# Finishing the first expert's down products before the second expert's rows are transposed

## The chip, the cores and the metric

The kernel runs on one core of a Trainium2 chip. The metric is the device time of one execution in microseconds; three executions of the kernel before gave a median of 880.13 us, from 878.72 to 883.2. The trace was taken in another, profiled execution of the same program.

The core has five engines that the text names as the profile does: PE (TensorE, matrix products and transposes; PEld are its weight loads), DVE (VectorE), ACT (ScalarE), POOL (GpSimd) and SP (SyncE, which here only issues transfers). Each engine works through its own list of instructions in order, and an instruction whose inputs are not there holds up everything behind it on that engine.

## The reference

The model is one layer over 512 tokens of width 1024: a mixer (three linear-attention branches), a layer norm, then a mixture of experts and a last layer norm. The change touches the mixture alone. A router takes two of 16 experts for each token (both from one of four groups of experts), and the sum of the two experts' outputs, each weighted, goes on:

```python
h = jax.nn.silu(jnp.einsum('td,edf->tef', t, w_gate)) * jnp.einsum('td,edf->tef', t, w_up)
y = jnp.einsum('tef,efd->td', h * combine[..., None].astype(h.dtype), w_down)
```

An expert has two matrices of 1024 x 256 (gate, up) and one of 256 x 1024 (down), in float32: 3 MB per expert.

## The kernel before

Everything is float32. A product of full precision is made from three products of split operands: each matrix is split into a high part (a rounding copy by ACT, `L321`) and a low part (the rest, a subtraction by DVE, `L322`), and `mm3` (`L337` to `L339`) multiplies high x high, high x low and low x high into the same PSUM bank. The third product is the only one that reads the low part of the left operand.

The expert loop begins at `L1639`. For each expert `e` there are 128 slots, each a token that chose it. Four things happen, in four functions:

- `slots_of` (`L1591`, by way of `slots`, `L1487`) finds which token sits in which slot: DVE makes one-hot matrices (`L1496`), PE multiplies them with a small table (`L1498`), and DVE makes the indices for reading and writing rows, `gidx` and `sidx` (`L1502` to `L1504`). What it returns, `rest`, makes the weights of the slots, `wsl`, from the same one-hots: four small products per expert (`L1510`) and one reduction (`L1511`).
- `gather` (`L1525`) reads the tokens' rows from the DRAM copy `h1d` into SBUF by an indirect transfer that POOL issues; `ex_in` (`L1536`) transposes them on PE (eight transposes, `L1541`), and `parts` splits each half into high (ACT, `L1533`) and low (DVE, `L1534`).
- `ex_up` (`L1545`) multiplies the rows with the gate and up matrices: four steps `u` of six products of 512 columns. After step `u` it calls `hook[u]`, if there is one.
- `ex_down` (`L1573`) takes the up products through `ex_hidden` (`L1560`: Silu on ACT, times the slot's weight on DVE, two transposes on PE, a split), multiplies with the down matrix (two splits, twelve products), copies the outcome to SBUF (ACT, `L1582`) and writes the rows to `y2d` by an indirect transfer (`L1583`).

The first expert's rows are not gathered: they are picked out of the norm's output by one-hot products (`rows0`). The second expert is the first one whose rows come through `h1d`, and its gather can't begin until the last block of `h1d` is written.

The loop runs one expert behind with the down products. In the turn of `e` it issues up(`e`), then the fetch of `e + 1` (the gather of the rows of `e + 2` and the transposes of the rows of `e + 1`), and then down(`e - 1`). In the first turn there is no down; down(0) comes in the second turn, after up(1) and the transposes of the third expert's rows.

The order on each engine is made by a planner: it takes the instructions in the order of the program, and where one is not ready by its own reckoning it may take a later one that is. Two things bind it. An instruction of a `Pinned` engine (`W` for DVE, `TP` for PE; all of them have the line `L149` in the profile) stays behind the instruction traced before it on that engine. What stands in `tc.issue_after(i)` stays behind `i`. In the first turn `TE` is `TP`, so all of PE's work of that turn is in the order of the program. The splits of the second expert's gate and up matrices stand behind `lows`, the last split of the first expert's rows (`L1551`). The splits of the first expert's down matrix have no such tie.

The split matrices go through rings of five buffers (`whs`, `wls`). A split has to wait until the products that read the buffer's former content are done. The first expert's third and fourth up matrices use the first two buffers; before the change the next four splits are the second expert's.

The hooks of the first three turns put the making of slots into the up products: `slots23` (slots of the third and fourth expert, and `weighs`, small DVE work on the router's weights) after step 2 of the first, `weights03` (slots of the first expert, which it needs for its down products alone, and all weights `wsl`) after step 1 of the second.

Of the kernel before, what the change touches and what calls it, by code (L numbers as in the profile page):

```python
# [38 lines left out]
def kernel(  # L39
# [6 lines left out]
    V, S, G, TE = nc.vector, nc.scalar, nc.gpsimd, nc.tensor  # L46
# [89 lines left out]
    def flat(a):  # L136
        return a.rearrange("p a b -> p (a b)")
# [13 lines left out]
    def pst(pool, shape=(P, T)):  # L151
        return pool.tile(list(shape), F32, name="ps")
# [4 lines left out]
    if True:  # L157
# [44 lines left out]
        W, X, TP, GP, Y = (Pinned(e) for e in (V, S, TE, G, nc.sync))  # L202
# [208 lines left out]
    def after(f):  # L411

        if act[0] is None:
            i = f()
        else:
            with tc.issue_after(act[0].ins):
                i = f()
        act[0] = i
        return i
# [550 lines left out]
    def weave(a, b=None, lead=0, more=0):  # L970


        res, live, i = [None, None], [a, b] if b else [a], 0
        while live:
            for g in list(live):
                if g is a or i >= lead or a not in live:
                    try:
                        res[g is b] = next(g)
                        if g is (b or a):
                            fill(more, 8)  # L980
                    except StopIteration:
                        live.remove(g)
            i += 1
        return res
# [112 lines left out]
    oA0, _ = weave(m0, more=2)  # L1097
# [19 lines left out]
    oC1, _ = weave(diag("C1", *q1[1], *f1[1], [vC1], False), more=4)  # L1117
# [4 lines left out]
    oB, _ = weave(diag("B", *fB[1], vB, True), more=4)  # L1122
# [19 lines left out]
    E = 16  # L1142
# [56 lines left out]
    def wo_unit(ch, u, *hl):  # L1199
        raw = raws((P, 2, T))  # L1200
        nc.sync.dma_start(raw, dram(w_out, D * 256 * u + 512 * ch, [[D, P], [D * P, 2], [1, 512]]))
        return split(raw, *hl)
# [184 lines left out]
    def rows0(q, n0, n1):  # L1387

        for n in range(n0, n1):
            for c in range(4):  # L1390
                TE.matmul(xps[q][:, c * P:(c + 1) * P], ah[n][:, (4 * q + c) * P:(4 * q + c + 1) * P], oh0[:, n],
                          start=n == 0 and c == 0, stop=n == NT - 1 and c == 3)
# [24 lines left out]
    late = [wo_unit(1, 2, *x4[:2]), wo_unit(1, 3, *x4[2:])]  # L1417
# [33 lines left out]
    half, logits, scores, rows, _ = lns[3]  # L1451
    xps += [pst(pp) for _ in range(2)]
    made = act[0]
    W, TP = Pinned(V), TE
# [61 lines left out]
    xgs = []  # L1516
# [14 lines left out]
    def parts(xT, q, ps, V=V):  # L1531
        qs = slice(4 * q, 4 * q + 4)
        S.copy(flat(xT[0][:, qs]), ps)  # L1533
        return V.tensor_sub(flat(xT[1][:, qs]), ps, flat(xT[0][:, qs]).bitcast(F32))  # L1534

    def ex_in(xg):  # L1536
        xT = [xTs((P, KD, P), F32R), xTs((P, KD, P), F32R)]
        for q in range(2):
            ps = pst(pm)
            for c in range(4):  # L1540
                TE.transpose(ps[:, c * P:(c + 1) * P], xg[:, (4 * q + c) * P:(4 * q + c + 1) * P], ident)  # L1541
            parts(xT, q, ps)
        return xT
# [16 lines left out]
    def ex_hidden(ps, wcol):  # L1560
        sg = scr()
        S.activation(sg[:, 0:256], ps[:, 0:256], AF.Silu)
        V.scalar_tensor_tensor(sg[:, 256:], ps[:, 256:], wcol, sg[:, 0:256], op0=ALU.mult, op1=ALU.mult)
        ps = pst(pm)
        for c in range(2):
            TE.transpose(ps[:, c * P:(c + 1) * P], sg[:, 256 + c * P:256 + (c + 1) * P], ident)
        mh = scrp.tile([P, 2, 2, P], F32R, name="mh", tag="scr", bufs=4)
        hT_ = [mh[:, 0], mh[:, 1]]
        S.copy(flat(hT_[0]), ps[:, :256])
        sub = V.tensor_sub(flat(hT_[1]), ps[:, :256], flat(hT_[0]).bitcast(F32))  # L1570
        return hT_, sub

    def ex_down(ps, raw, wcol, sidx_col, m=2 * T, e=0, hidden=None):  # L1573
        hT_, sub = hidden or ex_hidden(ps, wcol)
        yo = yos((P, D))
        ps = [pst(pp), pst(pp)]
        for k in range(2):
            w = split(raw[4 + k], V=G if e == E - 1 and k == 1 else V)
            for c in range(2):
                mm3(ps[c], lambda b, k: hT_[b][:, k], lambda b, k: w[b][:, c], k, k + 1, k == 0, k == 1)  # L1580
        for c in range(2):
            S.copy(yo[:, c * T:(c + 1) * T], ps[c])  # L1582
        s = nc.gpsimd.indirect_dma_start(  # L1583
            out=y2d[:m], out_offset=bass.IndirectOffsetOnAxis(ap=sidx_col, axis=0), in_=yo, in_offset=None,
            bounds_check=m - 1, oob_is_err=False)
        for o in scats:
            tc.declare_no_dep(s.ins, o.ins, reason="rows of other slots")
        scats.append(s)
        return sub

    def slots_of(e0, e1, V=V, mid=None):  # L1591
        es = slice(e0, e1)
        return slots(range(e0, e1), lambda e: pos[:, :, e:e + 1], lambda n, e: rc[:, n, e], gidx[:, es], sidx[:, es], wsl[:, es], V, mid)
# [3 lines left out]
    def fetch(e):  # L1597
        wts = weights(e) if e > 1 else first[e]
        if e % 4 == 1 and 1 < e < E - 4:
            slots_of(e + 3, e + 7)()  # L1600
        if e < E - 1:
            gather(xgs[(e + 1) % 3], gidx[:, e + 1:e + 2])
        return wts, ex_in(xgs[e % 3])


    first.append(weights(1))
    xT = [xTs((P, KD, P), F32R), xTs((P, KD, P), F32R)]
# [6 lines left out]
    def low(u):  # L1614
        W.tensor_sub(ready[u][1], first[0][u], ready[u][0].bitcast(F32))

    rows0(0, 2, 4)
    rest = [slots_of(1, 2, W, lambda: low(2))]
    rows0(1, 2, 4)
    parts(xT, 0, xps[0], W)  # L1620
    gather(xgs[1], gidx[:, 1:2])
    low(3)
    lows = parts(xT, 1, xps[1], W)
    wts = first[0]

    def slots23():
        rest.append(slots_of(2, 4, W))
        for f in weighs:
            f()

    def weights03():
        with tc.issue_after(lows.ins):
            rest.append(slots_of(0, 1))
        for f in rest:
            f()

    hooks = [{2: slots23}, {1: weights03}, {1: lambda: slots_of(4, 8)()}] + [{} for _ in range(E - 3)]
    late = None
    for e in range(E):  # L1639
        if e == E - 1:  # L1640
            ex_down(*late, e=e - 1)
        TE = TP if e == 0 else nc.tensor
        hid = []
        if 1 < e < E - 1:
            hooks[e][2] = lambda: hid.append(ex_hidden(late[0], late[2]))
        ps = ex_up(xT, wts, ready if e == 0 else (), e, hooks[e])
        done = late
        late = ps, wts, wsl[:, e:e + 1], sidx[:, e:e + 1]
        if e < E - 1:
            wts, xT = fetch(e + 1)  # L1650
        if 0 < e < E - 1:
            ex_down(*done, hidden=hid[0] if hid else None)
        TE = nc.tensor

# [31 lines left out]
    with tc.For_i(0, nmore, 1) as e:  # L1686
# [4 lines left out]
        wts = weights(e)  # L1691
# [18 lines left out]
    W = Pinned(V)  # L1710
# [84 lines left out]
```

## Time and profile before

| | us |
|---|---|
| median of three executions | 880.13 |
| the profiled execution | 884.35 |
| its span, first to last instruction | 882.6 |
| PE busy in it | 823.4 |
| DVE busy | 596.8 |
| ACT busy | 442.5 |

The page of the profile gives busy times over the whole span. The mixture of experts is the last fifth of it, from about 680 us on, so the views that matter are those with a window: the table of stretches, the order of instructions in time, and the chain of waits that ended last. Matmuls are pipelined, and the busy time of one is longer than its distance to the next.

### The profile page before, as it was taken

The page shows a single profiled execution, that of the slowest core. Times are in us where ns is not written, and L with a number is a line of the kernel's source. Part 1 is how long each engine was busy: PE and PEld are TensorE (multiplying, and loading weights), DVE is VectorE, ACT ScalarE, POOL GpSimd, SP SyncE. Part 2 cuts the span into 40 slices and gives each one's busy share as a digit, 9 for nine tenths or more (in the row PEclk, how much of TensorE's full clock was granted, in tenths as well). Part 3 has the DMA queues.
Part 4 walks back from the last instruction along what each step waited for, and adds up shares of the span by engine and source line. Part 5 has one row for each costly group of instructions (what it writes and reads, how often), then busy time and mean ns, then how long its engine had stood idle before and what let it go on. Part 6 is the DMA issues. An engine that isn't in the chain of part 4 may idle for free.

```text
span 882.6 us, 15196 instructions
## 1 busy us (share of the span) xinstructions
PE 823.4 (93%) x5860; PEld 692.9 (79%) x5860; DVE 596.8 (68%) x1104; ACT 442.5 (50%) x824; POOL 176.0 (20%) x197
## 2 busy tenths in 40 slices
PE   8989999999989999999999999999999799999930
PEld 5867878978887999988888888888777688888720
DVE  7775567787675655695934345545568799999838
ACT  6533456644465344374432223334223588989813
POOL 2560001440461330200100000000022133222332
PEclk9989999999999999999999999999999899999985
DMA  6512222022013221234524324335625899999452
GB/s 197 133 51 84 73 72 72 26 63 83 26 55 125 84 73 48 74 96 143 176 94 142 114 72 119 112 107 191 214 72 194 279 338 363 349 362 357 167 197 107
DMA packets 99999, 125.90 MB, mean 143 GB/s; under 512 B 12967, under 2 KB 86775, under 8 KB 99924
## 3 DMA queue, kind: packets, MB, share of 16 engines
q1 hardware_dynamic: 89344, 109.17, 37.5%
q10 hardware_dynamic: 6116, 7.48, 2.6%
q0 software_dynamic: 4464, 8.25, 2.5%
q8 instruction: 47, 0.77, 0.4%
q14 instruction: 28, 0.23, 0.1%
HBM read 118.21 MB, written 14.68 MB: 151 GB/s over the span
## 4 chain that ended last, share of the span: by engine, by line
PE 74%; DVE 10%; issue 5%; DMA 4%; ACT 4%; POOL 2%; DVEq 0%; SPq 0%; POOLq 0%; ACTq 0%
PE ps L337 19%; PE ps L339 19%; PE ps L338 19%; PE ps L149 5%; PE ps L911 1%; PE ps L1541 1%; DVE rr L322 1%; DMA y2d<-fl,sidx 1%; DMA ff<-y2d 1%; PE ps L939 1%; PE ps L656 1%; PE ps L941 1%; DMA fl<-h1d,gidx 1%; PE ps L898 1%; DVE ff L149 1%
## 5 line engine op out<-in xcount | busy, mean ns | idle before, releaser
L322 DVE TENSOR_TENSOR rr<-ff,rr 128x1024 fp32r<-128x1024 f32 x125 | 154.9, 1244 | 111.0 <-ACT rr L321 110.1
L321 ACT CAST rr<-ff 128x1024 fp32r<-128x1024 f32 x126 | 132.4, 1053 | 164.5 <-PE ps L338 126.1
L337 PE MATMUL ps<-rh,rr 128*128 128x512 f32 x384 | 153.7, 400 | 0.0
L338 PE MATMUL ps<-rh,rr 128*128 128x512 f32 x384 | 150.7, 392 | 0.0
L339 PE MATMUL ps<-rh,rr 128*128 128x512 f32 x384 | 150.6, 392 | 0.0
L337 PE MATMUL ps<-rr,rh 128*128 128x256 f32 (+1 forms) x320 | 93.3, 292 | 0.6 <-DVE rh L149 0.6
L339 PE MATMUL ps<-rr,rh 128*128 128x256 f32 (+1 forms) x320 | 91.8, 288 | 1.0 <-issue 1.0
L338 PE MATMUL ps<-rr,rh 128*128 128x256 f32 (+1 forms) x320 | 91.3, 286 | 0.0
L337 PEld LDWEIGHTS ps<-rh,rr 128*128 128x128 f32 x384 | 72.6, 189 | 15.4 <-issue 0.8
L339 PEld LDWEIGHTS ps<-rh,rr 128*128 128x128 f32 x384 | 72.5, 189 | 15.4
L338 PEld LDWEIGHTS ps<-rh,rr 128*128 128x128 f32 x384 | 72.6, 189 | 14.2
L337 PEld LDWEIGHTS ps<-rr,rh 128*128 128x128 f32 x320 | 61.0, 191 | 2.7 <-issue 1.4
L339 PEld LDWEIGHTS ps<-rr,rh 128*128 128x128 f32 x320 | 60.8, 191 | 1.4 <-issue 0.8
L338 PEld LDWEIGHTS ps<-rr,rh 128*128 128x128 f32 x320 | 61.1, 191 | 0.2
L1244 POOL TENSOR_TENSOR ff<-ff,ff 128x512 f32<-128x512 f32 x2 | 2.6, 1280 | 231.8 <-DVE ff L149 231.8
L1583 POOL DMA_INDIRECT y2d<-fl,sidx x16 | 27.6, 1727 | 64.1 <-ACT fl L1582 49.7
L339 PE MATMUL ps<-ro,rr 128*128 128x512 f32 x96 | 37.4, 389 | 0.0
L337 PE MATMUL ps<-ro,rr 128*128 128x512 f32 x96 | 37.3, 389 | 0.0
L338 PE MATMUL ps<-ro,rr 128*128 128x512 f32 x96 | 37.3, 389 | 0.0
L322 DVE TENSOR_TENSOR fr<-ff,fr 128x1024 fp32r<-128x1024 f32 x30 | 35.9, 1217 | 0.0
L321 ACT CAST fr<-ff 128x1024 fp32r<-128x1024 f32 x31 | 32.3, 1054 | 4.5 <-PE ps L339 3.3
L439 DVE SCALAR_TENSOR_TENSOR scr<-ps,vcol,scr 128x511 f32<-128x511 f32 (+2 forms) x36 | 26.7, 743 | 10.7 <-ACT scr L436 10.1
(594 smaller groups left out, 1779.5 us busy)
## 6 DMA issues: line engine op xcount, KB each, us to landing
ff<-in_w_in_dram SPq DMA_DIRECT2D x66, 512.0 KB
ff<-in_w_down_dram SPq DMA_DIRECT2D x26, 512.0 KB
ff<-in_w_gate_dram SPq DMA_DIRECT2D x48, 256.0 KB
ff<-in_w_up_dram SPq DMA_DIRECT2D x48, 256.0 KB
ff<-in_w_out_dram SPq DMA_DIRECT2D x8, 512.0 KB
ff<-y2d SPq DMA_DIRECT2D x6, 512.0 KB
fh<-in_w_gate_dram SPq DMA_DIRECT2D x11, 256.0 KB
fh<-in_w_up_dram SPq DMA_DIRECT2D x11, 256.0 KB
```

The costliest lines, as they stand in the source:

```text
L149: return lambda *a, **k: pin(f(*a, **k))
L321: S.copy(a, src)
L322: i = V.tensor_sub(b, src, a.bitcast(F32))
L337: TE.matmul(ps, w(0, k), h(0, k), start=start and k == k0, stop=False)
L338: TE.matmul(ps, w(0, k), h(1, k), start=False, stop=False)
L339: last = TE.matmul(ps, w(1, k), h(0, k), start=False, stop=stop and k == k1 - 1)
L439: V.scalar_tensor_tensor(y[:, sh:], ps[:, :T - sh], convw[:, j, j0:j0 + 1], y[:, sh:], op0=ALU.mult, op1=ALU.add)
L656: tiny = lambda ps, lhs, rhs: [TE.matmul(half(ps)[u, i], lhs[u, i], rhs[u, i], start=True, stop=True) for i in range(NL) for u in B32]
L898: TE.matmul(p4[:, :, n], kd[:, g * NT + n], qd[:, g * NT + n], start=True, stop=True)
L911: TE.matmul(ps[:, c], kd[:, c], qd[:, c], start=True, stop=True)
L939: TE.matmul(po, atv(h)[:, n], vs[h][:, n], start=True, stop=n == 0)
L1583: s = nc.gpsimd.indirect_dma_start(out=y2d[:m], out_offset=bass.IndirectOffsetOnAxis(ap=sidx_col, axis=0), in_=yo, in_offset=None, bounds_ ...
```

## The change

In the first turn the down products, with their copy to SBUF and the writing of the rows, now come after the up products of the first expert and ahead of the transposes of the second expert's rows. They are traced while `TE` is `TP`, so PE keeps this order. The second turn has no down products; from the third on the loop is as it was.

The slots of the first expert are made after step 1 of its own up products, together with `weighs`; its weights `wsl` after step 2; the slots of the third and fourth expert after step 3 instead of step 2. The weights of the second to fourth expert stay in the second turn. `fetch` no longer calls `ex_in`; the loop does. The table of ACT's functions that has Silu is loaded by an instruction of its own, ahead of the split of the first expert's rows.

```diff
-        return wts, ex_in(xgs[e % 3])
+        return wts
...
     rows0(1, 2, 4)
+    after(lambda: S.preload_act_table_set("silu_and_others"))
     parts(xT, 0, xps[0], W)
...
+    def slots0():
+        rest.append(slots_of(0, 1, W))
+        for f in weighs:
+            f()
+
     def slots23():
         rest.append(slots_of(2, 4, W))
-        for f in weighs:
-            f()
-
-    def weights03():
-        with tc.issue_after(lows.ins):
-            rest.append(slots_of(0, 1))
+
+    def weights13():
         for f in rest:
             f()
 
-    hooks = [{2: slots23}, {1: weights03}, {1: lambda: slots_of(4, 8)()}] + [{} for _ in range(E - 3)]
+    hooks = [{1: slots0, 2: lambda: rest.pop()(), 3: slots23}, {1: weights13}, {1: lambda: slots_of(4, 8)()}] + [{} for _ in range(E - 3)]
...
-        if e < E - 1:
-            wts, xT = fetch(e + 1)
-        if 0 < e < E - 1:
+        if e == 0:
+
+            wts = fetch(1)
+            ex_down(*late)
+            xT = ex_in(xgs[1])
+        elif e < E - 1:
+            wts = fetch(e + 1)
+            xT = ex_in(xgs[(e + 1) % 3])
+        if 1 < e < E - 1:
             ex_down(*done, hidden=hid[0] if hid else None)
```

## Rows read from the trace of the kernel before

**Rows 1.** The page's head: the span, and busy time of each engine with its share of the span.

```profile
span 882.6 us, 15196 instructions
PE 823.4 (93%) x5860; PEld 692.9 (79%) x5860; DVE 596.8 (68%) x1104; ACT 442.5 (50%) x824; POOL 176.0 (20%) x197
```

**Rows 2.** The table of stretches, from the end of the first expert's up products on. Columns: the stretch, its length, busy time and number of instructions of each engine, PE's granted clock (1.00 is 2.4 GHz, 0.50 is 1.2 GHz), the busy share of the DMA engines, GB/s.

```profile
689.80:693.10 3.30, 0.02 (x1) 0.02 (x1) 0.94 (x2) 1.11 (x2) 2.27 (x2) 0.92 1.03 376
693.10:703.50 10.40, 9.94 (x52) 7.70 (x53) 7.05 (x14) 5.28 (x6) 0.00 (x0) 0.70 0.70 241
703.50:715.40 11.90, 10.94 (x82) 8.96 (x81) 11.21 (x18) 8.76 (x13) 2.28 (x2) 1.00 0.94 330
...
715.40:820.30 104.90, 104.89 (x571) 86.67 (x570) 102.70 (x127) 94.67 (x132) 32.29 (x22) 1.00 1.00 355
```

**Rows 3.** The chain that ended last, around the second expert's gather. Columns: start in us, us, what.

```profile
684.63 7.66 DMA fl<-h1d,gidx
692.29 0.79 issue
693.08 1.97 PE ps L149 x8
```

**Rows 4.** The order in time from the end of the norm to the second expert's gathered rows. Columns: start, us, engine, line, operation, out<-in, and in brackets how long the engine was idle before and for what.

```profile
679.03 0.69 ACT L1305 ACTIVATE ff<-ps,rs1o 128x512 f32<-128x512 f32 x1 [0.17 <-PE ps L149]
...
679.62 1.03 ACT L321 CAST rr<-fh 128x1024 fp32r<-128x1024 f32 x1
...
682.03 0.59 ACT L1533 CAST ro<-ps 128x512 fp32r<-128x512 f32 x1 [1.37 <-PE ps L149]
...
688.14 1.63 PE L149 MATMUL ps<-rr,ro 128*128 128x512 f32 x6
...
689.24 1.28 ACT L1562 ACT_TABLE_LOAD   x1
...
690.30 1.28 POOL L1526 DMA_INDIRECT fl<-h1d,gidx  x1 [4.38 <-DVE gidx L149]
690.54 0.38 ACT L1562 ACTIVATE scr<-ps 128x256 f32<-128x256 f32 x1
```

**Rows 5.** The order in time, PE's rows that begin or follow a wait, up to the transposes of the fourth expert's rows.

```profile
693.08 1.97 PE L149 MATMUL ps<-ident,fl 128*128 128x128 f32 x8 [3.31 <-DMA fl<-h1d,gidx]
...
697.12 0.80 PE L339 MATMUL ps<-rr,ro 128*128 128x512 f32 x1 [0.32 <-DVE ro L1534]
...
703.50 1.03 PE L1541 MATMUL ps<-ident,fl 128*128 128x128 f32 x8
...
705.57 0.25 PE L1498 MATMUL ps<-rc,fl 128*128 128x3 bf16 x4 [0.73 <-DVE fl L1496]
...
706.05 0.50 PE L337 MATMUL ps<-rr,mh 128*128 128x512 f32 x1 [0.23 <-ACT mh L1569]
...
715.36 1.04 PE L1541 MATMUL ps<-ident,fl 128*128 128x128 f32 x8
```

**Rows 6.** The order in time at the last expert: from its last up product to its last down product.

```profile
842.61 0.39 PE L339 MATMUL ps<-rr,ro 128*128 128x512 f32 x1
843.04 0.38 ACT L1562 ACTIVATE scr<-ps 128x256 f32<-128x256 f32 x1 [2.47 <-PE ps L339]
843.46 0.48 DVE L1563 SCALAR_TENSOR_TENSOR scr<-ps,wsl,scr 128x256 f32<-128x256 f32 x1 [2.18 <-ACT scr L1562]
844.00 0.44 PE L1566 MATMUL ps<-ident,scr 128*128 128x128 f32 x2 [1.00 <-DVE scr L1563]
...
844.47 0.37 ACT L1569 CAST mh<-ps 128x256 fp32r<-128x256 f32 x1 [1.05 <-PE ps L1566]
...
844.89 0.50 PE L337 MATMUL ps<-rr,mh 128*128 128x512 f32 x1 [0.38 <-ACT mh L1569]
...
847.55 0.40 PE L339 MATMUL ps<-fr,mh 128*128 128x512 f32 x1
```

**Rows 7.** The table of stretches, columns as in rows 2, for PE's longest gaps, the work behind two of them, and the last expert's end.

```profile
57.60:61.60 4.00, 0.01 (x1) 0.00 (x0) 3.94 (x8) 0.00 (x0) 3.79 (x7) 0.94 0.43 131
61.60:67.80 6.20, 6.17 (x137) 4.89 (x138) 4.23 (x7) 1.33 (x3) 1.04 (x3) 0.50 0.28 87
255.10:257.50 2.40, 0.07 (x2) 0.01 (x1) 0.88 (x1) 2.03 (x9) 2.24 (x3) 1.00 0.00 0
...
693.00:699.00 6.00, 5.46 (x31) 4.23 (x32) 3.83 (x9) 2.12 (x3) 0.00 (x0) 0.50 0.79 288
842.00:848.00 6.00, 4.57 (x23) 3.10 (x21) 1.39 (x5) 1.34 (x3) 2.51 (x2) 1.00 0.53 187
```

**Rows 8.** The order in time on DVE during the router's work: a small operation of `weigh`, which the program traces later, and a wait of DVE for PE.

```profile
666.25 0.28 DVE L1266 TENSOR_TENSOR ga<-ga,ps 16x128 f32<-16x128 f32 x1 [0.57 <-PE ps L149]
...
676.64 0.18 DVE L1364 TENSOR_TENSOR scr<-sco,Mb 128x32 f32<-128x32 f32 x1
```

**Rows 9.** Groups of instructions, the first from 684.6 to 715.4 us and the others from 740 to 820 us. Columns: line, engine, operation, out<-in, count | busy us, mean ns of one | idle us of the engine before them, and what ended it.

```profile
L1502 DVE TENSOR_SCALAR slt<-ps 128x3 f32<-128x3 f32 (+1 forms) x2 | 0.3, 162 | 4.4 <-PE ps L1498 4.4
...
L322 DVE TENSOR_TENSOR rr<-ff,rr 128x1024 fp32r<-128x1024 f32 x23 | 27.5, 1216 | 0.0
L321 ACT CAST rr<-ff 128x1024 fp32r<-128x1024 f32 x24 | 25.0, 1057 | 2.9 <-PE ps L339 1.8 <-DMA ff<-in_w_up_dram 0.3 <-DVE rr L322 0.3
...
L1534 DVE TENSOR_TENSOR ro<-ps,ro 128x512 fp32r<-128x512 f32 x16 | 10.3, 684 | 0.4 <-issue 0.2 <-ACT ro L1533 0.2
```

## Prediction, made before the changed kernel was run

> **What bounds the kernel now.** The page comes first: PE is busy for 93% of the span, so the question is where it is not, or is slow [rows 1]. The table of stretches answers that for the mixture of experts. From 715.4 to 820.3 us PE works 104.89 of 104.9 us at the full clock; the twelve experts there can gain nothing but a shift. The 25.6 us before, from the first expert's last up product to the fourth expert's transposes at 715.36, hold only 20.9 us of PE work (0.02 + 9.94 + 10.94), and the clock is 0.70 in their middle part [rows 2]. The chain of waits names the cause: the gather of the second expert's rows is issued at 684.63, lands 7.66 us later, and the transposes begin at 693.08 [rows 3]. The order in time gives the gaps: 3.31 us for the gather, 0.32 for a split, 0.73 and 0.23 at 705 to 706 [rows 5].
>
> The clock adds to that. From 693 to 699 it is 0.50, 1.2 GHz, with 5.46 us of PE work in 6 us; before it fell PE had done nothing for 3.3 us [rows 7]. It was back at 1.00 by 700. With the 0.39 us or so up to its rise, some 5.85 us of work ran at half speed, which cost 2.9 us. So these 25.6 us hold 4.7 us of idle time and 2.9 us of slow work: 7.6 us is all that can be won here.
>
> What is won there reaches the end if nothing else binds the experts behind. ACT's splits wait for PE to free a buffer (1.8 us of their 2.9 us of waits) and for a weight's transfer only 0.3 us [rows 9]; the weights come early enough, and PE sets the pace.
>
> **The change part by part.** The mark is the begin of the fourth expert's transposes, 715.36 us: by then both kernels have done three up products, one down product and the same transposes, so a shift of the mark is a shift of the end.
>
> *Removed:* the whole 7.6 us, if PE has something to do while the gather lands. It has the down products: they need nothing of the gather.
>
> *Added, the uncovered hidden part.* Now nothing stands between the first expert's last up product and its down products. The last expert is in that position already. Its up products end at 843.00 (842.61 + 0.39); Silu, the weighting, two transposes and a rounding follow one another, and the first down product begins at 844.89. PE idles 1.00 + 0.38 us in it, 1.4 us. The last down product begins at 847.55, and with the distance of 0.23 us PE is free at 847.78, 4.8 us after the up products' end [rows 6]. There DVE had nothing else to do; here it has the splits of the down matrix and of the second expert's matrices, 1.22 us each [rows 9]. One of these ahead of the low part of the hidden values delays the third product, since PE's order is fixed. Bounds: 0, and 1.22 us; I take 0.4, because two products are in front of it (0.46 us) and ACT must first round the hidden values too.
>
> *Added, the transposes uncovered twice.* The second expert's transposes come straight before its up products, and so do the third's, since the second turn has no down products any more. In each case PE has to wait for ACT's rounding of the first half (0.59 us, rows 4) and DVE's subtraction (0.68 us, rows 9); four of the eight transposes and two products lie beside it (0.4 + 0.46 us). That leaves 0.4 us each, if ACT and DVE are free. They aren't: ACT also copies the down products' outcome, and DVE is in a split half of the time. I take 0.7 and 0.9 us, 1.6 us together. Bounds: 0.8 us, and with a split in front of each 3.2 us.
>
> *Moved, the slots.* The first expert's eight small products move from the second up products into the first, and the eight of the third and fourth expert from there to behind it, where PE would idle anyway. Count and duration are the same: 0 net. The gather of the third expert's rows, which began at 690.30 [rows 4], moves back by about one step, 1.4 us. With 7.7 us to landing [rows 3] and the 0.8 us after it the rows are there at some 700, and are wanted at some 703. That is hidden, with 3 us to spare; if the planner pulled those transposes forward PE would stand up to 2.4 us, and save the 0.9 us above. On POOL's list the first expert's write now stands ahead of the gather for the fourth expert, which isn't wanted before 711.
>
> *Moved, the table load.* It took 1.28 us at 689.24, in the wait, and Silu began at its end [rows 4]. Now it falls between 679.72 (the norm's last ACT instruction ends) and 682.03 (the rounding that waits for PE). In these 2.31 us ACT did one split of 1.03 us; 1.03 + 1.28 just fits, and the split can also go later. Cost 0, at most 0.3 us. The Trainium skill (ScalarE: Activation LUTs, What ACT_TABLE_LOAD costs) adds to 1.28 us a drain of 1.38 us, 2.66 us in all. By that page, as an estimate, the rounding would come 0.35 to 1.4 us late and the sum be 881.2 to 882.2. The row has 1.30 us from the load's begin to Silu's, without a drain, and the sum stays with it.
>
> *Freed, the down matrix's first split.* Its buffer was the second expert's before, and that split was tied behind `lows`. This one has no tie, its buffer is idle since the last products of the output projection, and the planner does put later work into DVE's gaps: `weigh` ran at 676.64 among the router's operations [rows 8]. A split of 1.22 us in a wait such as the 0.57 us at 666.25 [rows 8] delays a chain that ends in the first expert's up products. Bounds 0 and 1.22 us; I take the difference, 0.65.
>
> *The sum for the profiled execution:* 7.6 - 1.4 - 0.4 - 1.6 - 0.65 = 3.55 us off its 884.35 us, 880.8. Can DVE follow? It idled 4.4 us in one piece for PE's small products, in the gather's wait [rows 9], and 6 us in all up to the mark [rows 2]; a mark 3.6 us earlier leaves it 2 us. Just so.
>
> **From the profiled execution to the median.** The profiled execution took 4.2 us more than the median, and the three others lie 4.5 us apart. One stretch of half clock costs 2.9 us, and there is a like one at 61.6 us behind a gap of 4 us, while behind a gap of 2.4 us at 255 us the clock stayed [rows 7]. I take it that the fall at 693 belongs to about half of the executions. A kernel that avoids it then gains 3.55 - 1.45 = 2.1 us on the median: 880.13 - 2.1 = 878.0. Its own range is 876.6 (the fall in all executions) to 879.5 (in none).
>
> **The rivals.**
>
> *The clock gives nothing, 879.5.* Either the median execution had no fall, or the new gaps (1.0, 0.4, 0.7 us and the like within 8 us) make it fall all the same. Then 3.55 - 2.9 = 0.65 us is left. For it: the spread of the runs. Against the second form: at the last expert gaps of 1.0 and 0.38 us left the clock at 1.00 [rows 6, 7]. The Trainium skill (TensorE: Matmul & The Clock Gate, Part 1: The HAM clock gate) says that the same kernel meets the change of clock at another place from run to run, since the window runs freely. This speaks for the first form; one trace can't show it.
>
> *Everything fits, 874.9.* No split floats into the router's chain, none delays the hidden values, the transposes cost 0.8 us, and the median had the fall: 7.6 - 1.4 - 0.8 = 5.4 us, less a little for DVE, 5.2 us. For it: ACT is at 5 of 10 us there [rows 2]. Against it: DVE's 2 us would shrink to nothing.
>
> *DVE's list becomes the bound, 885.4, slower.* Between the first two up products DVE now has Silu's weighting, the hidden low part, two down splits, the rows' two low parts and up to four splits of the second expert. If a split of 1.22 us stands ahead of each of the four that PE waits for, that is 4.9 us, 4.5 beyond the 0.4 above; PE idles as long as in the old wait, the clock falls, 2.9 us more. 880.13 - 2.1 + 4.5 + 2.9 = 885.4. It decides against the change from 2.1 us of such queueing on. For it: DVE is at 11.2 of 11.9 us right behind [rows 2]. Against it: PE frees the split buffers late, so that not all four splits can be ready early.
>
> That the change doesn't do what it says is hardly a case: all of PE's work of the first turn is pinned, so the down products must come first.
>
> **How the numbers follow.** The forecast (878.0) gets 0.46, the clock that gives nothing 0.26, everything fits 0.14, DVE's list 0.14. The range from 874.5 to 882.7 holds the first three and the milder half of the last. Half a per cent, 4.4 us, is about what a measurement of this kernel can tell from no change: below 875.7 lie most of the third case and the best of the first, 0.24; above 884.5 the worse part of the last, 0.11; between them 0.65.
>
> **What would show it.** In the changed profile PE's longest gap near 690 should be about 1.0 us, before the two hidden transposes, the clock 1.00 through 690 to 700, the first down product some 2 to 3 us after the last up product, the second expert's transposes at 695 to 696 with no wait for the gather, and the fourth expert's transposes begin at 711 to 712.5 instead of 715.36. A float shows as an `L322` on DVE ahead of 680 and later up products of the first expert. The prediction is wrong if PE waits at the second or third expert's transposes for a transfer, if DVE's splits stand ahead of the hidden values, or if the clock falls again.

## The result, and the profile after

The changed kernel takes 886.6 us in the median of 20 executions (882.58 to 890.3); the kernel before, run beside it 20 times, takes 881.85 (878.72 to 886.18). The ratio is 1.0053, with a 95% interval from 1.0038 to 1.0069. The change costs 4.7 us. The forecast was 878.0, and its range ended at 882.7: the time rose where it was to fall, and lies outside the range.

The profiled execution took 889.78 us. The head of its page:

```profile
span 888.0 us, 15196 instructions
PE 826.4 (93%) x5860; PEld 696.7 (78%) x5860; DVE 596.3 (67%) x1104; ACT 442.4 (50%) x824; POOL 182.2 (21%) x197
```

As many instructions as before, and PE busy 3 us longer [rows 1]. The table of stretches, columns as in [rows 2], says where:

```profile
689.80:694.20 4.40, 4.35 (x26) 2.94 (x24) 3.73 (x9) 2.71 (x4) 0.00 (x0) 1.00 0.97 348
694.20:699.30 5.10, 4.12 (x23) 2.78 (x24) 4.54 (x10) 2.89 (x5) 1.76 (x2) 1.00 0.95 299
699.30:705.60 6.30, 2.08 (x24) 1.57 (x23) 4.56 (x7) 2.73 (x5) 1.91 (x2) 0.84 1.07 394
705.60:720.40 14.80, 14.80 (x88) 12.11 (x89) 10.28 (x16) 8.87 (x11) 3.28 (x2) 0.84 0.67 229
720.40:825.30 104.90, 104.83 (x571) 86.68 (x570) 102.37 (x127) 94.43 (x132) 34.48 (x21) 1.00 1.01 358
```

From the fourth expert's transposes on (720.43 here) the last row equals that of before: 104.83 us of work in 104.9. The stretch meant to be filled, 694.2 to 699.3, is filled but for 1.0 us (4.12 of 5.1). Behind it there is a new hole, 4.2 us in 6.3, with the clock at 0.84 in and behind it. The chain of waits reaches back only to 860.72 us here, so the hole is read from the order in time on PE:

```profile
687.99 3.00 PE L149 MATMUL ps<-fr,ro 128*128 128x512 f32 x12
...
694.81 0.25 PE L149 MATMUL ps<-rc,fl 128*128 128x3 bf16 x4 [0.35 <-DVE fl L149]
695.21 0.44 PE L149 MATMUL ps<-ident,scr 128*128 128x128 f32 x2
696.11 1.95 PE L149 MATMUL ps<-rr,mh 128*128 128x512 f32 x6 [0.46 <-ACT mh L1569]
697.89 1.56 PE L149 MATMUL ps<-fr,mh 128*128 128x512 f32 x6
699.29 1.04 PE L149 MATMUL ps<-ident,fl 128*128 128x128 f32 x8
700.16 0.45 PE L1510 MATMUL ps<-rc,fl 128*128 128x3 bf16 x12
700.65 0.50 PE L337 MATMUL ps<-fr,ro 128*128 128x512 f32 x1
700.99 0.40 PE L338 MATMUL ps<-fr,ro 128*128 128x512 f32 x1
705.57 0.87 PE L1541 MATMUL ps<-ident,fl 128*128 128x128 f32 x3 [4.18 <-DMA fl<-h1d,gidx]
...
706.66 0.63 PE L337 MATMUL ps<-fr,ro 128*128 128x512 f32 x1
...
713.16 0.71 PE L1541 MATMUL ps<-ident,fl 128*128 128x128 f32 x5
```

The first up product starts at 687.99. The second expert's transposes (699.29) wait for nothing: the gather that stopped PE for 3.31 us before [rows 3, 5] is hidden. But after two of the second expert's 24 up products stand three of the third expert's eight transposes, and PE waits 4.18 us for *their* gather. The order of the program has them after all 24; the planner pulled them forward. Behind the wait a product takes 0.63 us instead of 0.39: the clock is 0.50 until 710.35. A mean of 0.84 over 14.8 us at levels 1.00 and 0.50 means 4.7 us at half clock and 2.4 us lost. In this trace the late gather costs 4.2 + 2.4 = 6.6 us.

Why it is late shows on DVE, which makes the indices, and on POOL, which issues the gather. The order in time, DVE and then POOL:

```profile
689.50 0.68 DVE L149 TENSOR_TENSOR fl<-slot,pos 128x512 bf16<-128x512 f32 x1
690.86 1.23 DVE L322 TENSOR_TENSOR fr<-fh,fr 128x1024 fp32r<-128x1024 f32 x1 [0.67 <-ACT fr L321]
692.00 0.15 DVE L149 TENSOR_SCALAR slt<-ps 128x3 f32<-128x3 f32 x1
692.07 1.22 DVE L322 TENSOR_TENSOR fr<-fh,fr 128x1024 fp32r<-128x1024 f32 x1
693.21 0.15 DVE L149 SCALAR_TENSOR_TENSOR gidx<-slt 128x1 int32<-128x1 f32 x1
...
693.47 1.29 DVE L149 TENSOR_TENSOR fl<-slot,pos 128x512 bf16<-128x512 f32 x2
...
695.10 0.16 DVE L149 TENSOR_SCALAR slt<-ps 128x6 f32<-128x6 f32 x1
695.18 1.21 DVE L322 TENSOR_TENSOR rr<-ff,rr 128x1024 fp32r<-128x1024 f32 x1
696.32 0.15 DVE L149 SCALAR_TENSOR_TENSOR gidx<-slt 128x2 int32<-128x2 f32 x1
```

```profile
687.43 2.26 POOL L1526 DMA_INDIRECT fl<-h1d,gidx  x1 [9.24 <-DVE ro L149]
697.24 1.65 POOL L1526 DMA_INDIRECT fl<-h1d,gidx  x1 [7.55 <-DVE mh L1570]
```

The chain for the first expert's slot (one-hot matrix 689.50, `slt` 692.00, `gidx` 693.21) comes first; the one-hots of the third and fourth expert follow at 693.47. Three times a split of 1.2 us stands between two links (690.86, 692.07, 695.18), and ahead of the first of them DVE waits 0.67 us for ACT's part of it. The gather of the third expert's rows is issued at 697.24, 9.25 us after the first up product (687.99). Before, it was 690.30 [rows 4], 6.58 us after the first up product, which stood at 683.72:

```profile
683.72 3.01 PE L149 MATMUL ps<-fr,ro 128*128 128x512 f32 x12
```

Two more differences lie ahead of the first up product. The first split of the down matrix floated, and the router's chain pays. DVE, then PE:

```profile
667.16 0.15 DVE L187 TENSOR_SCALAR rs<-rs 128x1 int32<-128x1 int32 x1
667.22 1.22 DVE L322 TENSOR_TENSOR rr<-fh,rr 128x1024 fp32r<-128x1024 f32 x1
...
668.43 0.15 DVE L188 TENSOR_SCALAR rs<-rs 128x1 int32<-128x1 int32 x1
```

```profile
673.55 0.66 PE L149 MATMUL ps<-ident,ff 128*128 128x128 f32 x4 [2.01 <-DVE ff L149]
```

The split stands inside a chain of small operations (`rs`), and PE waits 2.01 us for its end; before, that wait was 1.25:

```profile
670.87 0.66 PE L149 MATMUL ps<-ident,ff 128*128 128x128 f32 x4 [1.25 <-DVE ff L149]
```

Also, the clock was 0.50 from 683.04 to 686.46, which the first profile of the kernel before does not have.

### The profile page after: what moved, and what is told of

It reads as the page before. It is cut to its first block, busy times and chain, and to the rows that moved or that the text cites. A ratio compares the mean times of both kernels' runs of the same rounds, so it can differ in the third digit from the quotient of the medians.

```text
span 888.0 us, 15196 instructions
## 1 busy us (share of the span) xinstructions
PE 826.4 (93%) x5860; PEld 696.7 (78%) x5860; DVE 596.3 (67%) x1104; ACT 442.4 (50%) x824; POOL 182.2 (21%) x197
## 5 line engine op out<-in xcount | busy, mean ns | idle before, releaser
L321 ACT CAST rr<-ff 128x1024 fp32r<-128x1024 f32 x128 | 134.4, 1053 | 165.8 <-PE ps L338 121.4
L1583 POOL DMA_INDIRECT y2d<-fl,sidx x16 | 30.7, 1921 | 46.6 <-ACT fl L1582 34.2
L322 DVE TENSOR_TENSOR fr<-ff,fr 128x1024 fp32r<-128x1024 f32 x28 | 33.4, 1215 | 5.4 <-ACT fr L321 5.4
L321 ACT CAST fr<-ff 128x1024 fp32r<-128x1024 f32 x29 | 30.2, 1054 | 10.0 <-PE ps L339 9.2
L1526 POOL DMA_INDIRECT fl<-h1d,gidx x15 | 20.0, 1332 | 72.9 <-PE ps L1541 40.4
```

Source lines behind the costliest of these rows:

```text
L321: S.copy(a, src)
L322: i = V.tensor_sub(b, src, a.bitcast(F32))
L1526: return nc.gpsimd.indirect_dma_start(out=dst, out_offset=None, in_=h1d, in_offset=bass.IndirectOffsetOnAxis(ap=idx, axis=0), bounds_check ...
L1583: s = nc.gpsimd.indirect_dma_start(out=y2d[:m], out_offset=bass.IndirectOffsetOnAxis(ap=sidx_col, axis=0), in_=yo, in_offset=None, bounds_ ...
```

## The experiments

Nine kernels were timed against the kernel before, 12 executions each; the unchanged kernels were traced three more times, one execution each. The table gives the median and its ratio, and from one trace of each five times in us. "Head" is the time from the first `h1d` store to the first up product, "middle" from there to the fifth expert's transposes (724.71 before), "gather" the issue of the third expert's gather after the first up product, "wait" PE's wait at the third expert's rows. From the fifth expert's transposes to the start of the last down product it is 122.7 to 122.9 us in all 14 traces.

| kernel | median | ratio to before, 95% | head | middle | sum | gather | wait |
|---|---|---|---|---|---|---|---|
| before, first profile | 881.85 | | 29.68 | 40.99 | 70.67 | 6.58 | 0 |
| after | 886.6 | 1.0038 to 1.0069 | 32.03 | 41.79 | 73.82 | 9.25 | 4.18 |
| e1_hold | 881.8 | 0.9974 to 1.0016 | 32.07 | 36.04 | 68.11 | 9.26 | 0 |
| e2_slots2 | 885.19 | 1.0017 to 1.0059 | 33.59 | 39.56 | 73.15 | 9.42 | 0 |
| e3_tie | 882.97 | 0.9980 to 1.0025 | 31.31 | 40.56 | 71.87 | 8.61 | 2.92 |
| e4_all | 883.41 | 0.9984 to 1.0027 | 29.69 | 39.56 | 69.25 | 9.35 | 0 |
| e5_swap | 883.26 | 0.9989 to 1.0036 | 32.05 | 38.78 | 70.83 | 6.14 | 0 |
| e6_hold_tie | 881.52 | 0.9969 to 1.0009 | 31.30 | 36.53 | 67.83 | 8.61 | 0 |
| e7_swap_hold_tie | 884.96 | 1.0008 to 1.0050 | 29.68 | 42.41 | 72.09 | 5.98 | 0 |
| e8_before_filled | 881.97 | 0.9975 to 1.0018 | 29.69 | 37.27 | 66.96 | 6.58 | 0 |
| e9, before again | one execution | | 31.29 | 36.69 | 67.98 | 6.58 | 0 |
| e10, after again | one execution | | 33.66 | 41.99 | 75.65 | 9.25 | 4.92 |
| e11_fill_router | 881.87 | 0.9974 to 1.0013 | 29.68 | 36.58 | 66.26 | 8.61 | 0 |
| e12, before again | one execution | | 29.69 | 38.08 | 67.77 | 6.58 | 0 |

The kernel before had medians of 881.6 (35 executions, e1 to e4), 881.15 (35, e5 to e8) and 882.16 (17, e9 to e12).

**Is it the late gather?** e1_hold leaves everything of the change and keeps the third expert's transposes behind the second's last up product.

```diff
+            lastmm[0] = mm3(ps, ...)
...
-            xT = ex_in(xgs[(e + 1) % 3])
+            if e == 1:
+                with tc.issue_after(lastmm[0].ins):
+                    xT = ex_in(xgs[2])
+            else:
+                xT = ex_in(xgs[(e + 1) % 3])
```

> The changed kernel, with the transposes of the third expert's rows held behind the last up product of the second expert. Theory A (three of these transposes were pulled into the second expert's up products and stand there for a gather that now starts late): the 4.2 us gap of PE before them goes, and with it the fall of the clock behind it (2.9 us); a wait of some 0.7 us comes back before the third expert's up products. So 5 to 6 us less than the changed kernel, about equal to the kernel before (-1 to +1 us). Theory B (the loss is the first down split standing in the router's chain, and the clock's fall behind that): 0 to 1 us less than the changed kernel, 4 us slower than before. Theory C (DVE's list is the bound): PE waits as long at another place, no change.

The median is 881.8, 4.8 us below that of the changed kernel and a little less than theory A's 5 to 6, and the middle is 5.75 us shorter. On PE, all eight transposes now come after the last up product, with no wait:

```profile
704.15 0.39 PE L339 MATMUL ps<-rr,ro 128*128 128x512 f32 x1
704.39 1.03 PE L1541 MATMUL ps<-ident,fl 128*128 128x128 f32 x8
```

The gather was issued as late as in the changed kernel, 9.26 us after the first up product at 685.88:

```profile
695.14 1.65 POOL L1526 DMA_INDIRECT fl<-h1d,gidx  x1 [7.35 <-DVE mh L1572]
```

So the late gather alone costs nothing; late gather and pulled transposes together cost all that the change loses.

**What makes the gather late?** e2_slots2 makes the slots of the third and fourth expert one step earlier.

```diff
-    hooks = [{1: slots0, 2: lambda: rest.pop()(), 3: slots23}, ...
+    hooks = [{1: slots0, 2: lambda: (rest.pop()(), slots23())}, ...
```

> The changed kernel, with the slots of the third and fourth expert made after step 2 of the first up products again, as before the change. Theory A: the gather of the third expert's rows starts 2 to 2.5 us earlier against the first up products, the gap before the pulled transposes shrinks from 4.2 to about 2 us, and the clock may then hold: 2 to 5 us less than the changed kernel. Theory B: no change. Theory C: no change, or slower by some tenths, since DVE makes these one-hots earlier.

The median is 1.4 us below that of the changed kernel (885.19), not the 2 to 5 of theory A, and the gather came no earlier (9.42). PE waits for the one-hots instead, and the down products come later too (700.00, 11.1 us after the first up product against 8.1):

```profile
695.14 0.25 PE L149 MATMUL ps<-rc,fl 128*128 128x3 bf16 x4 [1.53 <-DVE fl L149]
...
700.00 2.93 PE L149 MATMUL ps<-rr,mh 128*128 128x512 f32 x6 [0.46 <-ACT mh L1569]
```

So the step at which PE has its place for the small products is not what holds the gather back; DVE's list is. e5_swap exchanges the order on that list.

```diff
-    hooks = [{1: slots0, 2: lambda: rest.pop()(), 3: slots23}, ...
+    hooks = [{1: slots23, 2: slots0, 3: lambda: rest.pop()()}, ...
```

> The changed kernel with the two slot steps exchanged: the slots of the third and fourth expert after step 1 of the first up products, the first expert's slots after step 2, its weights after step 3. Theory A (the first expert's slots, which DVE has to finish first, made the third expert's gather late): the gather is issued about 6.5 us after the first up product instead of 9.25, PE's wait at the pulled transposes falls from 4.18 us to about 1.3, the clock stays at 1.00 there, and the median is 882 or below instead of 886.6. Theory B (the gather is late because DVE is full of splits in that stretch, whatever the order of the slots): issued at 8.5 us or later, the wait stays above 3 us, the median is 885 or more.

On DVE, the one-hots of the third and fourth expert now come first, and their indices are there 5.2 us after the first up product (686.66) instead of 8.3:

```profile
688.17 1.28 DVE L149 TENSOR_TENSOR fl<-slot,pos 128x512 bf16<-128x512 f32 x2
...
691.88 0.15 DVE L149 SCALAR_TENSOR_TENSOR gidx<-slt 128x2 int32<-128x2 f32 x1
```

The gather is issued 6.14 us after the first up product, and the pulled transposes (703.49) wait for nothing:

```profile
692.80 2.05 POOL L1526 DMA_INDIRECT fl<-h1d,gidx  x1 [4.22 <-DVE gidx L149]
```

So the first expert's slots ahead on DVE had made it late. But now PE waits for the first expert's:

```profile
692.88 0.25 PE L149 MATMUL ps<-rc,fl 128*128 128x3 bf16 x4 [1.54 <-DVE fl L149]
...
696.06 0.41 PE L149 MATMUL ps<-ident,scr 128*128 128x128 f32 x2 [1.34 <-DVE scr L1563]
```

Of 4.18 us of wait, 2.9 came back in these two, the clock fell behind them (0.50 from 698.14 to 701.55, where 1.00 was expected), and the median is 883.26, above the 882 that was expected. In neither of the two orders are both chains early: both go through DVE between splits of 1.2 us.

**What does the floating split cost?** e3_tie keeps both down splits of the first expert behind `lows`.

```diff
-            w = split(raw[4 + k], V=G if e == E - 1 and k == 1 else V)
+            if tied:
+                with tc.issue_after(lows.ins):
+                    w = split(raw[4 + k])
...
-            ex_down(*late)
+            ex_down(*late, tied=True)
```

> The changed kernel, with both splits of the first expert's down matrix tied behind the last split of the first expert's rows, as the second expert's splits are. Theory A: only the split's own share, 0.8 us, goes. Theory B: 0.8 us and the clock's fall at 683 us (1.7 us), 2.5 us or more. Theory C: slower than the changed kernel by up to 1 us, since DVE has one split more between the two up products.

The router's wait is 1.25 us again, 0.76 less. The tie brought more than that in the median (882.97 against 886.6), the size that theory B had given (2.5 us or more). But theory B's reason isn't shown: the trace has a low clock ahead of the first up product too, from 679.18 to 682.59. What the trace shows is that the gather came 0.64 us earlier: three splits stand between the links here too, but the first is ready when its turn comes, and DVE's wait of 0.67 us is gone. The wait at the third expert's rows is 2.92 instead of 4.18:

```profile
701.88 0.52 PE L1541 MATMUL ps<-ident,fl 128*128 128x128 f32 x3 [2.92 <-DMA fl<-h1d,gidx]
```

The tied splits made a wait of 1.43 us at the hidden values, though. Head and middle together are 1.95 us shorter than in the changed kernel's trace; where the rest of the 3.6 us in the medians comes from stays open.

**All three together:** e4_all has the edits of e1, e2 and e3.

> All three edits together: transposes held, slots of the third and fourth expert after step 2, down splits tied. Theory A: the waits are gone, 6 to 7 us less than the changed kernel, 1 to 3 us faster than the kernel before. Theory B: equal to the tied kernel. Theory C: not faster than the kernel before.

883.41: the parts don't add up. The step of e2 makes its waits for one-hots here too (0.93 and 0.35 us), PE waits 1.08 and 0.33 us more for DVE at the hidden values, and the clock is 0.50 from 697.02 to 700.43. e6_hold_tie leaves that step out.

> The changed kernel with the third expert's transposes held behind the second's up products (as in e1_hold) and both down splits of the first expert tied behind the last split of its rows (as in e3_tie). If the gains are separate: the router's gap of 2.01 us goes back to about 1.25, the stretch from the first h1d store to the first up product is about 31.3 us or less, and the median is 881.8 - 0.7 = 881.1 or below. If the tie's gain in e3_tie came only from the shorter wait at the gather: no gain left, 881.8, and the tied splits are late at the down products (a gap above 0.5 us before the first down products).

881.52, within 0.4 us of the kernel before and of e1_hold: the router's 0.75 us came back, and the tied splits gave most of it away again (1.44 us of wait at the hidden values, where the changed kernel has 0.14, and 0.35 at the one-hots ahead of them). e7_swap_hold_tie adds the exchange of e5.

> The exchange of e5_swap with the hold and the tie of e6_hold_tie. Theory A: with the transposes held, the gather has time enough either way, so the exchange adds nothing: within 0.5 us of e6_hold_tie. Rival: the exchange also takes DVE's chain out of the way of the hidden values' weights or puts it there; then the gap before the two hidden transposes (0.35 to 1.0 us so far) changes by the same amount as the time, 1 us either way.

It missed both ways, 3.4 us slower: PE waits 2.39 us for the first expert's one-hots and 1.34 for its hidden values, the clock is 0.50 from 692.14 to 702.38, and the middle is 42.41 us, the longest of all. With the transposes held nobody needs an early gather, so the exchange only has its price.

**What was there to win?** Three more traces show that the profile of before was not a typical execution. e8_before_filled puts 13 spare products into the old wait.

```diff
+        if e == 1:
+            spare = pst(pm)
+            for n in range(13):
+                TE.matmul(spare..., onb, onb..., start=True, stop=True)
         return wts, ex_in(xgs[e % 3])
```

> The kernel before, with 13 spare products of 128x512 (onb x onb, into a PSUM tile that nobody reads, some 2.8 us) ahead of the second expert's transposes, where PE stood 3.31 us for the gather. Theory A (half of the executions lose 2.9 us to the lower clock behind this wait, as the prediction took it): the granted clock behind the gather is 1.00, PE's gap below 1 us, the median falls by about 1.5 us against the kernel before, and the runs above 884 become rare. Rival B (the fall belongs to few executions, or the two groups of times of the kernel before come from elsewhere): the median stays within 0.5 us and the runs still form two groups.

PE works through the old wait, and the clock stays at 1.00 until 847. In order of time, and then the stretch of the transposes:

```profile
689.72 2.98 PE L149 MATMUL ps<-onb 128*128 128x512 bf16 x13
692.53 1.04 PE L149 MATMUL ps<-ident,fl 128*128 128x128 f32 x8
```

```profile
692.50:698.50 6.00, 5.94 (x47) 4.74 (x46) 5.17 (x13) 3.18 (x4) 0.47 (x1) 1.00 1.06 380
```

The median didn't fall (881.97 against 881.15), but no execution of 12 lay above 884 (highest 883.34), against 8 of 35 of the kernel before beside it. e9 and e12 are the kernel before, unchanged, traced again.

> The kernel before, one more profiled execution. Theory B' (only a quarter to a third of its executions meet the lower clock behind the gather's wait, 8 of 35 lay above 884 us in one comparison and 11 of 35 in another): with about two chances in three the granted clock is 1.00 from 690 to 715 us and the span is about 878.5 to 879.5. Rival (half or more, as the prediction took it): an even chance that the clock falls again within a few us of the wait, with a span near 882.6.

> The kernel before once more, for the same question as e9_before_again: two chances in three of the clock at 1.00 behind the gather's wait by theory B', one in two by the rival.

PE at the second expert's transposes, and the stretch behind, in e9:

```profile
693.32 1.09 PE L149 MATMUL ps<-ident,fl 128*128 128x128 f32 x8 [0.91 <-DMA fl<-h1d,gidx]
```

```profile
693.30:699.30 6.00, 5.01 (x41) 3.86 (x42) 4.45 (x12) 3.51 (x6) 1.92 (x2) 1.00 0.98 352
```

And in e12:

```profile
693.79 1.09 PE L149 MATMUL ps<-ident,fl 128*128 128x128 f32 x8 [2.29 <-DMA fl<-h1d,gidx]
```

```profile
693.80:699.80 6.00, 5.02 (x42) 3.87 (x43) 4.40 (x10) 3.32 (x5) 0.79 (x1) 1.00 0.92 327
```

The wait is 0.91 and 2.29 us instead of 3.31, and the clock behind it is 1.00 both times, where the first profile had 0.50 [rows 7]. The spans, 881.6 and 880.8 us, are longer than expected. e9 has half clock elsewhere, from 681.15 to 684.57; both have it for 3.4 us more, from 257.90 and from 259.34, behind the gap of 2.33 us where the first profile kept 1.00 [rows 7]; and the time behind the start of the last down product differs by up to 1.2 us. Over all comparisons 27 of 107 executions of the kernel before took 884 us or more, as its first profiled one did (884.35), and none of the 48 of e1, e6, e8 and e11, in which no wait of over 1.5 us is left from the first up product to the fifth expert's transposes. That fits a fall of the clock behind the gather's wait in about a quarter of the executions. An execution without a trace tells its mean clock alone, so that each of the 27 is of this kind isn't shown.

**Is the changed kernel's wait always there?** e10 is the changed kernel, traced again.

> The changed kernel, one more profiled execution. Theory A: PE's wait at the third expert's pulled transposes comes from the order of instructions and is there again, 3.5 to 4.5 us, with the gather issued 9 us or more after the first up product; the clock may fall or not, the span is 881 to 888. Rival: the wait of 4.18 us was of this one execution (a slow gather), and is below 2 us.

The wait is 4.92 us, more than the 4.5 that were expected at most, with the gather 9.25 us after the first up product and the clock at 0.50 from 703.17 to 710.00:

```profile
706.42 0.87 PE L1541 MATMUL ps<-ident,fl 128*128 128x128 f32 x3 [4.92 <-DMA fl<-h1d,gidx]
```

It is the same picture in both traces, and e1_hold showed that it comes from the order.

**The low clock near 680.** e6 spends 5.6 us from the start of the last `h1d` store to the first up product, 4.0 in e8. e11_fill_router fills the router's wait of 1.26 us, ahead of it, with spare products.

> e6_hold_tie with five spare products of 128x512 (about 1.1 us, into a PSUM tile that nobody reads) in PE's wait of 1.26 us in the router, ahead of the last block's second transposes. Theory: the lower clock of 3.4 us near 680 in e6_hold_tie, which makes the stretch from the last h1d store to the first up product 5.6 us instead of 4.0, comes from that wait; with PE at work it stays at 1.00, and the median falls by up to 1.6 us, to 880, below both kernels. Rival: the clock falls there for another reason, or in few executions only: 881.5, no change.

The stretch behind, in e6 and then in e11:

```profile
681.00:686.00 5.00, 5.00 (x35) 4.99 (x35) 3.38 (x12) 1.42 (x2) 0.20 (x1) 0.69 0.92 303
```

```profile
681.00:686.00 5.00, 5.00 (x53) 4.95 (x50) 4.73 (x15) 2.58 (x4) 0.00 (x0) 1.00 1.05 360
```

In the profile the clock stayed up and the head was 1.6 us shorter, but the median didn't move (881.87 against 881.52). The kernel before has this low clock in one trace of three (e9), with the wait of 1.25 us in all three. So it comes in some executions and not in others, and the fill's effect isn't shown. Over all traces it goes with the wait, though: all five with the floated split and its wait of 2.01 us (both of the changed kernel, e1, e2, e5) have a low clock between the first `h1d` store and the first up product, and of the eight with the wait of 1.25 us left unfilled three do (e9, e3, e6). So few traces don't settle it.

No version beats the kernel before by more than can be measured here; e6_hold_tie and e11_fill_router come closest (0.9969 to 1.0009 and 0.9974 to 1.0013).

## Why the prediction was wrong

**The step that failed** is the one on the slots: "The gather of the third expert's rows, which began at 690.30 [rows 4], moves back by about one step, 1.4 us ... That is hidden, with 3 us to spare; if the planner pulled those transposes forward PE would stand up to 2.4 us, and save the 0.9 us above." Both halves failed. The gather moved back by 2.67 us against the first up product (9.25 - 6.58), because the step was counted on PE, where the small products have their place, and not on DVE, where the one-hots queue behind another expert's chain with its two splits, and meet a third. And the planner did pull the transposes forward, which the text priced and then dropped: with 9.25 us to the issue, 8.33 from there to the transposes (705.57 - 697.24) and PE ready for them 13.40 after the first up product (705.57 - 4.18 - 687.99), PE stands 9.25 + 8.33 - 13.40 = 4.18 us. The price of 2.4, for which the text gives no working, had the issue 1.3 us earlier, and it had no fall of the clock behind the wait, another 2.4. What the prediction counted as 0 was 6.6 (6.7 in e10: 4.92 of wait, and 3.6 us of work at half clock). A wait at the third expert's transposes and a fall of the clock are two of the signs that the prediction named for its being wrong.

**The second failure is the size of what could be won.** Of the 7.6 us [rows 2, 5, 7], 2.9 were low clock. (It fell at 692.56, 2.8 us into PE's wait and not, as the prediction reads, behind 3.3 us of it.) The prediction took that for half of the executions, 1.45 us; a quarter would give 0.7. And the wait of 3.31 us is 0.91 and 2.29 in the other two traces: it ends with the gather. In e9 PE lost 1.6 us to a low clock at 681, so that the gather was issued 1.28 us sooner against the first up product; it also took 1.13 us less, and PE waited 2.4 us less. In e12 the two are 0.47 and 0.54 us. The gaps from there to the fifth expert's transposes add up to 2.8 us in e9 (0.91, 0.15, 0.82, 0.88, 0.07) and 4.2 in e12, not 4.7. So the rival "The clock gives nothing, 879.5" was right about the kernel before, in two of its three traces.

**The base** was low as well: the 880.13 us of three executions are 881.85 in 20. Of the 8.6 us between forecast and measurement 1.7 lie in the base, and have nothing to do with the change.

**The rivals.** "DVE's list becomes the bound, 885.4" had the nearest time and the right engine, at 0.14, and with it a wait as long as the old one and a fall of the clock; but what came late was not a split that PE waits for; it was an index, and through it a transfer. That PE frees the split buffers late, the argument against it, does not bear on the index chain.

**What was right.** PE's order, and the second expert's transposes without a wait. The uncovered hidden part: the gaps are 0.35 + 0.14 + 0.46 = 0.95 us against 1.4, since small products of the slots fill some of it, and the first down product begins 1.9 us after the small products behind the last up product (694.21). The float: 0.76 us against 0.65. Over the mark: 0.02 us for the low part of the hidden values instead of 0.4, and 0.04 and 0.20 us (the latter in e1_hold) for the two uncovered sets of transposes instead of 1.6. The weights' small products lie between transposes and up products (700.16 above), and cover the roundings.

The table load delayed nothing that PE waited for, as said:

```profile
682.42 1.28 ACT L1620 ACT_TABLE_LOAD   x1
...
686.09 0.59 ACT L1533 CAST ro<-ps 128x512 fp32r<-128x512 f32 x1 [2.39 <-PE ps L149]
```

ACT ends it at 683.70 and then waits 2.39 us for PE. The trace shows the 1.28. The 2.66 us of the Trainium skill (ScalarE: Activation LUTs, What ACT_TABLE_LOAD costs) would have fitted here too.

**The sum with measured terms**, against e12: the new waits are 1.1 us (0.35, 0.14, 0.46, 0.06, 0.04, 0.02), the late gather 6.6, and e12's 4.2 us of gaps go: 3.5 us longer, and the middle is 3.7 longer (41.79 - 38.08). The head is 2.34 longer (32.03 - 29.69): 0.76 for the float, the other 1.6 the low clock at 683, of which it isn't shown how much is the change's. Without that clock the sum is 4.3 us (3.5 + 0.76), with it 5.8; the measured 4.7 lies between. Without the late gather the change would gain 4.2 - 1.1 - 0.76 = 2.3 us on e12 and 0.9 on e9. e1_hold is that kernel: 881.8 against 881.6, and its interval reaches from 2.3 us faster to 1.4 slower, so that even this gain isn't shown. Its trace has the low clock ahead of the first up product too, from 680.51 to 683.92; if the float makes that more frequent, it takes back part of the gain.

## What to carry to other kernels

When a producer of indices is moved, follow it through every engine's list to the transfer that it issues, and look for the consumer of that transfer wherever the planner may put it: a margin worked out from the program's order holds only if the order is fixed. Ask of a wait that is to be filled how long it is in other executions, and whether delays ahead of it already vanish in it; trace the unchanged kernel more than once before counting what can be won.

## What the runs showed of the hardware

The kernel before, traced three times, had its low clock behind the gather (692.56), ahead of it (681.15), and in neither place. The Trainium skill (TensorE: Matmul & The Clock Gate, Part 1: The HAM clock gate) says of a kernel's begin that the place of the change varies from run to run; the three traces show that it does in mid-kernel too. Which of these an execution meets is worth 1.6 to 2.9 us here, about as much as the change itself was to bring.

A place that no edit touched shows it best. All 14 traces have a gap of 2.33 or 2.34 us on PE, ending between 256.6 and 259.0 us. Behind it the clock was 0.50 for 3.4 us in nine of them and stayed at 1.00 in five, among them the first trace of the kernel before [rows 7], by which the prediction judged such gaps.

An indirect read of 128 rows of 4 KB took 7.3 to 9.1 us from its issue to the transposes that waited for it (693.32 - 686.00 in e9, 693.08 - 684.63 in [rows 3], 706.42 - 697.36 in e10), with the transfer engines busy for 0.76 of the time or more. The Trainium skill (DMA: Bandwidth & Descriptors, Anatomy of one DMA — SWDGE (gpsimd) path) has a fit of 2.0 us plus the bytes at 436 GB/s, as an estimate 3.2 us for 512 KB. The six waits that were traced are all longer than twice that; with the weights' transfers beside it, the measured time is the one to count with.
